# Moving work between VectorE, GpSimd and ScalarE in two mixers of a four-layer network

## The chip, the cores and the metric

The kernel runs on one core of a Trainium2 chip. The metric is the device time of one execution in microseconds, the median of several runs. The engines are TensorE (PE in the profile; PEld is its weight loading), VectorE (DVE), ScalarE (ACT), GpSimd (POOL) and SyncE (SP), which here only issues DMAs. Each runs its own queue of instructions in order and waits on semaphores for the others.

## What is computed

A sequence of 512 tokens of width 1024 passes through four layers in float32. The first two are a block with a gated linear recurrence, then a stick-breaking attention, each followed by a gated feed-forward network; the last two are attention layers with a memory. The change touches the first and the third mixer. Cut to these:

```python
def _rglru_mixer(h, w_in, conv_w, conv_b, w_r, b_r, w_i, b_i, lam, w_out):   # first mixer
    proj = h @ w_in
    gate = gelu(proj[..., :1024], approximate=True)
    xc = causal_depthwise_conv(proj[..., 1024:], conv_w, conv_b)              # four taps
    xg = xc.reshape(bsz, s, 4, 256)
    r = sigmoid(einsum("bsnc,ncd->bsnd", xg, w_r) + b_r)
    i = sigmoid(einsum("bsnc,ncd->bsnd", xg, w_i) + b_i)
    log_a = 8.0 * r * log_sigmoid(lam)
    u = sqrt(maximum(-expm1(2.0 * log_a), 0.0)) * (i * xc)
    hs = linear_scan(exp(log_a), u)
    return (hs * gate) @ w_out

# third mixer: h @ w_in_even gives queries, keys, values of three attentions and a gate
ya = global_gqa(rope(rmsnorm(qa)), rope(rmsnorm(ka)), va)      # 8 heads, 2 key heads
yb = window_gqa(qb, kb, vb, sink_b, rel_bias)                  # 8 heads, 2 key heads
ym = memory_attn(qm, mk, mv)                                   # 4 heads
x = x + (concatenate([ya, yb, ym]) * silu(gate)) @ w_out_even  # each attention: softmax(scores) @ v
```

## The kernel before

Activations lie transposed: a tile is 128 features by 512 tokens. A float32 product is made of three fp32r matmuls: each operand is split into a high part (rounded to fp32r, by ACT) and a low part (operand minus high part), and `mm3` (lines 169 to 171) multiplies high by high, high by low and low by high. A projection of one tile of 128 output features is 24 such matmuls of 512 columns, from two chunks of weights of 128x512.

Weights come through `fetch` (lines 139 to 155): a plan lists all chunks of the whole kernel in the order of their use; the DMA of a chunk goes to one of three buffers `w32`, ACT makes the high part `wh` (line 150), DVE the low part `wl` (line 151), each in one of six buffers. So a chunk can be prepared only up to six chunks ahead of its use, when PE has read the one that had its buffer. The instructions of each engine stand in an order that the framework's scheduler sets from the program; the order within an engine is fixed when the kernel is built.

The first mixer is `rglru`. `RG_STEPS` sets the order of its steps. A step `x` projects two tiles, scales them (DVE, line 423), and convolves each: the first tap by POOL (line 426), three more by DVE (line 429), then a split whose low part POOL makes (line 206). A step `g` multiplies a pair by the two gate matrices (24 matmuls), and then goes between ACT (tanh, exp, square; lines 450 to 463), DVE (lines 462, 464), POOL (maximum with zero, line 465), ACT (square root, with its table load, line 469) and DVE (line 472 and the scan, line 473). A step `y` is a gate tile: a projection, scaled by DVE (479), then the gelu: square on ACT (482), a multiply and add on POOL (483), a product on DVE (484), tanh on ACT (485), and two products on DVE (486, 489), the second with the scan's result; the split's low part is POOL's. The output projection follows with the first seven of the eight tiles, then the eighth.

The third mixer is `even_mixer`. The column tiles of its input weights `we_m` are numbered by `even_col`: 0 is the key of the global attention, 1 to 4 its queries, 5 the key and 6 to 9 the queries of the window attention, 10 to 13 the memory queries, 14 to 17, 18 to 21 and 22 to 25 the gates of the three. A query tile holds two heads. It passes the rope (`rope`; its last addition is POOL's, line 1074), is split (ACT line 204, POOL line 206), and four DMAs stack high and low parts for the score matmuls (lines 551, 552). `gqa_score` computes four blocks of scores per head, their maxima (DVE), the exponentials with their sums (ACT), and `normalise` (lines 961 to 965) multiplies each block by the reciprocal of its sum: four DVE instructions of 128x512 a head. `win_score` does the same with blocks of 256, 384, 384 and 256 columns. PE then transposes the normalised blocks, ACT and DVE split them (lines 620, 621), and PE multiplies them by the values. While a pair of heads is in its softmax, PE projects the next query and a gate tile.

Of the kernel before, what the change touches and what calls it, by code (L numbers as in the profile page):

```python
# [9 lines left out]
F32 = mybir.dt.float32  # L10
F32R = mybir.dt.float32r
BF16 = mybir.dt.bfloat16
AF = mybir.ActivationFunctionType
ALU = mybir.AluOpType
# [51 lines left out]
class Net:  # L66
# [73 lines left out]
    def fetch(self):  # L140
        nc = self.nc
        key, c0, c1 = self.plan[self.fetched]
        self.fetched += 1
        n = c1 - c0
        src = self.a[key[0]][key[1:]][:, c0:c1]
        w = self.w32.get()
        h = self.wh.get()
        l = self.wl.get()
        nc.sync.dma_start(w[:, :n], src)
        nc.scalar.copy(h[:, :n], w[:, :n])  # L150
        nc.vector.tensor_tensor(l[:, :n], w[:, :n], h[:, :n].bitcast(F32), op=ALU.subtract)  # L151
        self.w32.put(w)
        self.wh.put(h)
        self.wl.put(l)
        self.ready.append((key, c0, h, l))

    def weights(self, key, c0=0):

# [212 lines left out]
    def plan_rglru(self):  # L371
# [15 lines left out]
            self.chunks(("w_rgo", k), kd)  # L387

    RG_STEPS = [
        ("x", 0), ("x", 1), ("g", 0), ("x", 2), ("g", 1), ("x", 3), ("g", 2), ("y", 0), ("y", 1),  # L390
        ("g", 3), ("y", 2), ("y", 3), ("y", 4), ("y", 5), ("y", 6), ("y", 7),
    ]

    def first_pair(self, st):
# [15 lines left out]
    def rglru(self, st, gain_next):  # L410
        nc = self.nc
        v, act, pool = nc.vector, nc.scalar, nc.gpsimd
        c = self.scr
        first = deque(self.first_pair(st))
        YH, YL, conv, hs = [], [], {}, {}
        for kind, n in self.RG_STEPS:
            if kind == "x":
                xcs, ch, cl = [], [], []
                for mt in range(2):
                    m = 2 * n + mt  # L420
                    ps = first.popleft() if first else self.proj(("w_rg", 8 + m), st["XH"], st["XL"])
                    xbt, xb = self.f()
                    v.tensor_tensor(xb, ps, self.row(st), op=ALU.mult)
                    self.P.put(ps)
                    xct, xc = self.f()
                    pool.tensor_scalar(xc, xb, self.p("conv_w", 24 + m), self.p("conv_b", m), op0=ALU.mult, op1=ALU.add)
                    for j in (2, 1, 0):
                        d = 3 - j
                        v.scalar_tensor_tensor(xc[:, d:], xb[:, : 512 - d], self.p("conv_w", 8 * j + m), xc[:, d:], op0=ALU.mult, op1=ALU.add)
                    self.F.put(xbt)  # L430
                    xcs.append((xct, xc))
                    h, l = self.split(xc, "p")
                    ch.append(h)
                    cl.append(l)
                conv[n] = xcs, ch, cl
                if n == 0:
                    self.lam_consts()
            elif kind == "g":
                xcs, ch, cl = conv.pop(n)
                tr = []  # L440
                for g in range(2):
                    wh, wl = self.weights(("w_gate4", n), 512 * g)
                    for mt in range(2):
                        m = 2 * n + mt
                        ps = self.P.get()
                        for kt in range(2):
                            s = slice((mt * 2 + kt) * 128, (mt * 2 + kt + 1) * 128)
                            self.mm3(ps, wh[:, s], wl[:, s], ch[kt], cl[kt], kt == 0, kt == 1)
                        tt, t = self.f()
                        act.activation(t, ps, AF.Tanh, scale=0.5, bias=c[:, 16 + 8 * g + m : 17 + 8 * g + m])  # L450
                        self.P.put(ps)
                        tr.append((tt, t))
                self.R.put(*ch, *cl)
                keep = []
                for mt in range(2):
                    m = 2 * n + mt
                    (rt, r), (it, i) = tr[mt], tr[2 + mt]
                    xct, xc = xcs[mt]
                    at, aa = self.f()
                    act.activation(aa, r, AF.Exp, scale=c[:, m : m + 1], bias=c[:, m : m + 1])  # L460
                    act.activation(r, r, AF.Tanh, scale=c[:, 8 + m : 9 + m], bias=c[:, 8 + m : 9 + m])
                    v.scalar_tensor_tensor(i, i, 1.0, xc, op0=ALU.add, op1=ALU.mult)
                    act.square(xc, aa)
                    v.scalar_tensor_tensor(r, xc, 1.0, r, op0=ALU.add, op1=ALU.mult)
                    pool.tensor_scalar(r, r, 0.0, None, op0=ALU.max)
                    self.F.put(xct)
                    keep.append((m, at, rt, it))
                for m, at, rt, it in keep:
                    act.sqrt(rt[:, 0:512], rt[:, 0:512])
                for m, at, rt, it in keep:  # L470
                    r, i = rt[:, 0:512], it[:, 0:512]
                    v.scalar_tensor_tensor(i, i, 0.5, r, op0=ALU.mult, op1=ALU.mult)
                    v.tensor_tensor_scan(r, at[:, 0:512], i, 0.0, op0=ALU.mult, op1=ALU.add)
                    self.F.put(at, it)
                    hs[m] = rt
            else:
                ps = self.proj(("w_rg", n), st["XH"], st["XL"])
                gt, g = self.f()
                v.tensor_tensor(g, ps, self.row(st), op=ALU.mult)
                self.P.put(ps)  # L480
                qt, q = self.f()
                act.square(q, g)
                pool.tensor_scalar(q, q, 0.044715, 1.0, op0=ALU.mult, op1=ALU.add)
                v.tensor_tensor(q, q, g, op=ALU.mult)
                act.activation(q, q, AF.Tanh, scale=0.7978845608028654)
                v.scalar_tensor_tensor(g, q, 1.0, g, op0=ALU.add, op1=ALU.mult)
                self.F.put(qt)
                ht = hs.pop(n)
                v.scalar_tensor_tensor(g, g, 0.5, ht[:, 0:512], op0=ALU.mult, op1=ALU.mult)
                self.F.put(ht)  # L490
                yh, yl = self.split(g, "p")
                self.F.put(gt)
                YH.append(yh)
                YL.append(yl)
# [463 lines left out]
        self.F.put(qt)  # L958
        return hl

    def normalise(self, pieces, sums):
        nc = self.nc
        nc.vector.reciprocal(sums, sums)  # L963
        for c, x in pieces:
            nc.vector.tensor_scalar(x, x, sums[:, c : c + 1], None, op0=ALU.mult)  # L965

    def mem_score(self, q, K):
        nc = self.nc
# [153 lines left out]
    def gqa_score(self, Q, K, r8, hd):  # L1122
        nc = self.nc
        sums = self.small(4)
        tiles, pieces = [], []
        for b in range(4):
# [10 lines left out]
            self.P.put(ps)  # L1137
            tiles.append(t)
            pieces.append((b, p))
        self.normalise(pieces, sums)  # L1140
        return tiles, [x for _, x in pieces]

    def gqa_value(self, W, V):
# [41 lines left out]
    def win_score(self, Q, K, hd):  # L1185

        nc = self.nc
# [26 lines left out]
        es = self.small(4)  # L1214
        nc.scalar.activation(es, neg, AF.Exp, bias=sink)
        nc.vector.tensor_tensor(sums, sums, es, op=ALU.add)
        self.normalise(list(enumerate(xs)), sums)
        return tiles, xs

    def win_value(self, W, V):  # L1220
# [636 lines left out]
```

## Time and profile before

| | before |
|---|---|
| median of 3 runs | 1899.28 us (1898.69 to 1900.81) |
| profiled execution | 1898.13 us, of which the span of the instructions is 1896.1 us |
| PE busy | 1855.3 us, 98% of the span |
| DVE busy | 1204.7 us, 64% |
| ACT busy | 882.5 us, 47% |
| POOL busy | 318.5 us, 17% |

The first mixer lasts until about 153 us after the span's start, the third from about 1200 to 1455 us. PE is busy nearly always, so a change is worth what it does to the short times in which PE isn't, or in which it runs slower. The shares are averages over the whole kernel: in the two mixers DVE is far fuller than 64%.

### The profile page before, as it was taken

How to read it: one execution, taken by the hardware profiler on the slowest of the kernel's cores; microseconds unless marked ns; L12 is line 12 of the kernel's file. 1: busy time of each engine (PE TensorE's matmuls, PEld its weight loads, DVE VectorE, ACT ScalarE, POOL GpSimd, SP SyncE). 2: the span in 40 equal slices, each digit the busy share in tenths (PEclk: the TensorE clock that was granted, in tenths of full speed). 3: DMA queues.
4: the chain of work that ended last, by engine and by line, in shares of the span. 5: the costliest groups of instructions: out<-in, count | busy, mean ns of one | idle time of the engine just before them, and what ended most of it. 6: DMA issues, size and time to landing. Idle time of an engine off the chain costs nothing. (4 is left out here: it accounts for less than half of the span.)

```text
span 1896.1 us, 25818 instructions
## 1 busy us (share of the span) xinstructions
PE 1855.3 (98%) x9003; PEld 1545.3 (81%) x9003; DVE 1204.7 (64%) x2181; ACT 882.5 (47%) x1709; POOL 318.5 (17%) x370
## 2 busy tenths in 40 slices
PE   9899999999999999999999999999999999999998
PEld 6777888888888888788888888788888888888877
DVE  8886555553335998655554335779897665776753
ACT  5764333333334665533333344456665444545542
POOL 3342000000001221200000131222212411322310
PEclk9999999999999999999999999999999999999999
DMA  5333333333335442333333334322443433545532
GB/s 157 101 106 106 95 99 96 97 97 97 94 95 161 135 139 78 94 96 98 97 97 103 104 114 145 89 73 62 112 113 95 129 96 98 145 138 144 142 95 73
DMA packets 124802, 204.04 MB, mean 108 GB/s; under 512 B 21208, under 2 KB 31192, under 8 KB 124672
## 3 DMA queue, kind: packets, MB, share of 16 engines
q1 hardware_dynamic: 124672, 202.39, 37.0%
q8 instruction: 71, 1.16, 0.3%
q14 instruction: 59, 0.48, 0.1%
HBM read 168.76 MB, written 4.40 MB: 91 GB/s over the span
## 5 line engine op out<-in xcount | busy, mean ns | idle before, releaser
L171 PE MATMUL p<-r,wl 128*128 128x512 f32 (+1 forms) x2216 | 853.7, 385 | 10.3 <-DVE wl L151 10.3
L169 PE MATMUL p<-r,wh 128*128 128x512 f32 (+1 forms) x2216 | 856.9, 387 | 2.0 <-ACT wh L150 1.4
L170 PE MATMUL p<-r,wh 128*128 128x512 f32 (+1 forms) x2216 | 852.7, 385 | 3.0 <-POOL r L206 2.2
L150 ACT CAST wh<-w 128x512 fp32r<-128x512 f32 x608 | 371.4, 616 | 643.3 <-PE p L170 480.3
L151 DVE TENSOR_TENSOR wl<-w,wh 128x512 fp32r<-128x512 f32 x608 | 439.9, 727 | 339.4 <-ACT wh L150 337.0
L171 PEld LDWEIGHTS p<-r,wl 128*128 128x128 f32 x2216 | 417.2, 188 | 96.3 <-DVE wl L151 13.9
L169 PEld LDWEIGHTS p<-r,wh 128*128 128x128 f32 x2216 | 417.0, 188 | 86.0 <-ACT wh L150 4.0
L170 PEld LDWEIGHTS p<-r,wh 128*128 128x128 f32 x2216 | 417.3, 188 | 85.6 <-POOL r L206 4.3
L206 POOL TENSOR_TENSOR r<-f,r 128x512 fp32r<-128x512 f32 x102 | 139.5, 1369 | 455.5 <-ACT r L204 454.7
L204 ACT CAST r<-f 128x512 fp32r<-128x512 f32 x146 | 90.7, 621 | 186.2 <-DVE f L532 65.3
L220 POOL TENSOR_TENSOR f<-f,f 128x512 f32<-128x512 f32 x40 | 56.2, 1412 | 478.2 <-ACT f L214 478.0
L506 DVE TENSOR_TENSOR f<-p,f 128x512 f32<-128x512 f32 x68 | 46.9, 690 | 83.5 <-PE p L171 82.8
L621 DVE TENSOR_TENSOR r<-p,r 128x512 fp32r<-128x512 f32 (+2 forms) x152 | 90.4, 638 | 3.7 <-ACT r L620 3.4
L620 ACT CAST r<-p 128x512 fp32r<-128x512 f32 (+2 forms) x152 | 77.2, 558 | 10.5 <-PE p L1152 5.4
L597 PE MATMUL p<-wh,r 128*128 128x512 f32 (+1 forms) x192 | 71.7, 374 | 0.6 <-DVE f L610 0.6
L599 PE MATMUL p<-wh,r 128*128 128x512 f32 (+1 forms) x192 | 71.4, 372 | 0.0
L598 PE MATMUL p<-wl,r 128*128 128x512 f32 (+1 forms) x192 | 71.3, 372 | 0.0
L530 DVE TENSOR_TENSOR f<-p,f 128x512 f32<-128x512 f32 x44 | 30.4, 691 | 63.6 <-PE p L171 63.6
L509 ACT ACTIVATE f<-f 128x512 f32<-128x512 f32 x68 | 43.0, 633 | 38.6 <-DVE f L506 38.5
L682 POOL MEMSET f<- 128x1 f32 x64 | 5.2, 99 | 313.9 <-DVE f L510 208.3
L965 DVE TENSOR_SCALAR f<-f,s 128x256 f32<-128x256 f32 (+3 forms) x160 | 56.5, 416 | 1.1
L683 DVE TENSOR_TENSOR_SCAN f<-f,f 128x127 f32<-128x127 f32 (+3 forms) x64 | 53.1, 870 | 6.3 <-ACT f L676 6.3
(214 smaller groups left out, 1852.9 us busy)
## 6 DMA issues: line engine op xcount, KB each, us to landing
w<-w_gu SPq DMA_DIRECT2D x176, 256.0 KB, 2.9
r<-r SPq DMA_DIRECT2D x240, 128.0 KB, 2.5
w<-w_d SPq DMA_DIRECT2D x80, 256.0 KB, 2.7
w<-wo_m SPq DMA_DIRECT2D x64, 256.0 KB, 2.9
w<-we_m SPq DMA_DIRECT2D x52, 256.0 KB, 2.9
w<-w_rg SPq DMA_DIRECT2D x32, 256.0 KB, 3.0
w<-w_sqk SPq DMA_DIRECT2D x32, 256.0 KB, 2.9
w<-we_o SPq DMA_DIRECT2D x24, 256.0 KB, 2.6
```

Source lines behind the costliest of these rows:

```text
L150: nc.scalar.copy(h[:, :n], w[:, :n])
L151: nc.vector.tensor_tensor(l[:, :n], w[:, :n], h[:, :n].bitcast(F32), op=ALU.subtract)
L169: mm(out, wh, xh, start=start, stop=False)
L170: mm(out, wh, xl, start=False, stop=False)
L171: mm(out, wl, xh, start=False, stop=stop)
L204: nc.scalar.copy(h, src)
L206: e.tensor_tensor(l, src, h.bitcast(F32), op=ALU.subtract)
L597: mm(o, xh, h[:, s], start=st, stop=False)
L598: mm(o, xh, l[:, s], start=False, stop=False)
L599: mm(o, xl, h[:, s], start=False, stop=sp)
L620: nc.scalar.copy(h[:, :n], ps[:, :n])
L621: nc.vector.tensor_tensor(l[:, :n], ps[:, :n], h[:, :n].bitcast(F32), op=ALU.subtract)
```

## The change

Four things. In the first mixer the first tap of the convolution is made by ACT (`Identity` with a scale and a bias for each partition) instead of POOL. The gelu's multiply and add leave POOL: the factor 0.044715 goes into the scale of ACT's square, and the addition of one into DVE's product, which becomes a scalar_tensor_tensor. `RG_STEPS` puts gate tiles between the other steps. In the third mixer the low parts of the weights of column tiles 1 to 9 and 18 to 25 are made by POOL instead of DVE, and one of four blocks of each head is normalised by ACT.

```diff
@@ fetch
-        nc.vector.tensor_tensor(l[:, :n], w[:, :n], h[:, :n].bitcast(F32), op=ALU.subtract)
+        e = nc.gpsimd if self.low_on_pool(key) else nc.vector
+        e.tensor_tensor(l[:, :n], w[:, :n], h[:, :n].bitcast(F32), op=ALU.subtract)
...
+    @staticmethod
+    def low_on_pool(key):
+
+        return key[0] == "we_m" and (1 <= key[1] <= 9 or key[1] >= 18)
@@ RG_STEPS
-        ("x", 0), ("x", 1), ("g", 0), ("x", 2), ("g", 1), ("x", 3), ("g", 2), ("y", 0), ("y", 1),
-        ("g", 3), ("y", 2), ("y", 3), ("y", 4), ("y", 5), ("y", 6), ("y", 7),
+        ("x", 0), ("x", 1), ("g", 0), ("y", 0), ("x", 2), ("g", 1), ("y", 1), ("y", 2), ("x", 3),
+        ("g", 2), ("y", 3), ("y", 4), ("g", 3), ("y", 5), ("y", 6), ("y", 7),
@@ rglru, step x
-                    pool.tensor_scalar(xc, xb, self.p("conv_w", 24 + m), self.p("conv_b", m), op0=ALU.mult, op1=ALU.add)
+                    act.activation(xc, xb, AF.Identity, scale=self.p("conv_w", 24 + m), bias=self.p("conv_b", m))
@@ rglru, step y
-                act.square(q, g)
-                pool.tensor_scalar(q, q, 0.044715, 1.0, op0=ALU.mult, op1=ALU.add)
-                v.tensor_tensor(q, q, g, op=ALU.mult)
+                act.activation(q, g, AF.Square, scale=0.044715**0.5)
+                v.scalar_tensor_tensor(q, q, 1.0, g, op0=ALU.add, op1=ALU.mult)
@@ normalise
-    def normalise(self, pieces, sums):
+    def normalise(self, pieces, sums, act=None):
...
-            nc.vector.tensor_scalar(x, x, sums[:, c : c + 1], None, op0=ALU.mult)
+            if c == act:
+                nc.scalar.activation(x, x, AF.Copy, scale=sums[:, c : c + 1])
+            else:
+                nc.vector.tensor_scalar(x, x, sums[:, c : c + 1], None, op0=ALU.mult)
@@ gqa_score
-        self.normalise(pieces, sums)
+        self.normalise(pieces, sums, 3)
@@ win_score
-        self.normalise(list(enumerate(xs)), sums)
+        self.normalise(list(enumerate(xs)), sums, 2)
```

Lines stand further down in the changed kernel: one or two in `fetch`, five or six in `rglru`, eight in the rope.

The order of the queues moves with it. First DVE in the first mixer, where the first step `g` ends. Before, with the taps of `x` 2 among it (line 423 the evacuation, 429 the taps, 464, 472 and 473 the gate instructions and scans, `wl` the weights' low parts):

```order
L423 TENSOR_TENSOR f_210<-p_116,f_212 128x512
L429 SCALAR_TENSOR_TENSOR f_211<-f_210,par,f_211 128x511
L464 SCALAR_TENSOR_TENSOR f_202<-f_213,f_202 128x512
L429 SCALAR_TENSOR_TENSOR f_211<-f_210,par,f_211 128x510
L464 SCALAR_TENSOR_TENSOR f_205<-f_215,f_205 128x512
L429 SCALAR_TENSOR_TENSOR f_211<-f_210,par,f_211 128x509
L151 TENSOR_TENSOR wl_234<-w_2_222,wh_228 128x512
L151 TENSOR_TENSOR wl_229<-w_0_220,wh_223 128x512
L472 SCALAR_TENSOR_TENSOR f_206<-f_206,f_202 128x512
L472 SCALAR_TENSOR_TENSOR f_207<-f_207,f_205 128x512
L473 SCALAR_TENSOR_TENSOR f_202<-f_208,f_206 128x512
L473 SCALAR_TENSOR_TENSOR f_205<-f_209,f_207 128x512
```

In the changed kernel (470, 478, 479 are the gate instructions and scans, 429 the evacuation of `x`, 435 its taps, 485, 489, 491 and 494 a gate tile):

```order
L485 TENSOR_TENSOR f_210<-p_116,f_212 128x512
L470 SCALAR_TENSOR_TENSOR f_202<-f_213,f_202 128x512
L470 SCALAR_TENSOR_TENSOR f_205<-f_215,f_205 128x512
L489 SCALAR_TENSOR_TENSOR f_211<-f_211,f_210 128x512
L478 SCALAR_TENSOR_TENSOR f_206<-f_206,f_202 128x512
L478 SCALAR_TENSOR_TENSOR f_207<-f_207,f_205 128x512
L479 SCALAR_TENSOR_TENSOR f_202<-f_208,f_206 128x512
L479 SCALAR_TENSOR_TENSOR f_205<-f_209,f_207 128x512
L429 TENSOR_TENSOR f_204<-p_117,f_212 128x512
L491 SCALAR_TENSOR_TENSOR f_210<-f_211,f_210 128x512
L152 TENSOR_TENSOR wl_234<-w_2_222,wh_228 128x512
L494 SCALAR_TENSOR_TENSOR f_210<-f_210,f_202 128x512
```

The first gate tile's instructions stand where taps of `x` 2 stood, the evacuation of `x` 2 follows the scans, and its taps come further down, with `wl` between them.

Then POOL in the third mixer, at the second and third query tiles of the global attention. Before (1074 the rope's addition, 206 the low parts of a query and of an output, 239 a power for the norm):

```order
L1074 TENSOR_TENSOR f_218<-f_218,f_209 128x512
L206 TENSOR_TENSOR r_166<-f_218,r_177 128x512
L239 TENSOR_TENSOR s_106<-s_105,mhalf 128x8
L206 TENSOR_TENSOR r_154<-f_209,r_155 128x512
L1074 TENSOR_TENSOR f_207<-f_207,f_203 128x512
```

In the changed kernel (1082, 212 and 245 are the same three, 152 the weights' low parts):

```order
L1082 TENSOR_TENSOR f_217<-f_217,f_203 128x512
L152 TENSOR_TENSOR wl_230<-w_1_221,wh_224 128x512
L152 TENSOR_TENSOR wl_231<-w_2_222,wh_225 128x512
L212 TENSOR_TENSOR r_158<-f_217,r_177 128x512
L152 TENSOR_TENSOR wl_232<-w_0_220,wh_226 128x512
L245 TENSOR_TENSOR s_106<-s_105,mhalf 128x8
L212 TENSOR_TENSOR r_154<-f_203,r_155 128x512
L152 TENSOR_TENSOR wl_233<-w_1_221,wh_227 128x512
L1082 TENSOR_TENSOR f_216<-f_216,f_204 128x512
```

Four low parts of weights a query stand on POOL, two of them here between the rope's addition and the query's low part.

## Rows read from the trace of the kernel before

**Rows 1.** Windows: stretch, length, busy us (instructions) of PE, PEld, DVE, ACT, POOL; PEclk

```profile
25.00:150.00 125.00, 115.38 (x489) 91.95 (x488) 106.73 (x155) 80.25 (x128) 52.73 (x40) 0.99 0.33 99
79.00:82.50 3.50, 3.50 (x10) 2.70 (x9) 2.59 (x5) 2.13 (x4) 1.27 (x2) 0.51 0.72 195
1258.00:1432.00 174.00, 168.46 (x881) 140.41 (x879) 162.44 (x383) 111.47 (x266) 35.74 (x25) 1.00 0.33 91
```

**Rows 2.** Waits of PE, 25 to 153 us: us in total, times, longest

```profile
PE p L171 <- DVE wl L151: 6.9, 4, 3.7
PE p L170 <- POOL r L206: 1.9, 2, 1.0
```

**Rows 3.** Timeline of PE: start, us, what, [idle before <- who ended it]

```profile
78.05 0.50 PE L171 MATMUL p<-r,wl 128*128 128x512 f32 x1 [3.69 <-DVE wl L151]
...
79.55 0.63 PE L170 MATMUL p<-r,wh 128*128 128x512 f32 x1
79.98 0.63 PE L171 MATMUL p<-r,wl 128*128 128x512 f32 x1
```

**Rows 4.** Waits of DVE, 25 to 150 us

```profile
DVE f L429 <- POOL f L426: 6.6, 8, 2.0
DVE f L484 <- POOL f L483: 3.4, 4, 1.9
DVE f L464 <- ACT f L463: 2.4, 4, 0.8
DVE f L472 <- ACT f L469: 2.1, 3, 1.0
```

**Rows 5.** Timeline of DVE in the first mixer

```profile
73.21 0.75 DVE L429 SCALAR_TENSOR_TENSOR f<-f,par,f 128x511 f32<-128x511 f32 x1 [2.00 <-POOL f L426]
...
75.08 2.33 DVE L473 TENSOR_TENSOR_SCAN f<-f,f 128x512 f32<-128x512 f32 x2
77.33 0.67 DVE L151 TENSOR_TENSOR wl<-w,wh 128x512 fp32r<-128x512 f32 x1
...
82.03 1.76 DVE L429 SCALAR_TENSOR_TENSOR f<-f,par,f 128x511 f32<-128x511 f32 x1 [0.91 <-POOL f L426]
...
98.44 1.28 DVE L151 TENSOR_TENSOR wl<-w,wh 128x512 fp32r<-128x512 f32 x2
...
124.73 1.10 DVE L489 SCALAR_TENSOR_TENSOR f<-f,f 128x512 f32<-128x512 f32 x1
```

**Rows 6.** Timeline of POOL in the first mixer

```profile
81.96 1.29 POOL L206 TENSOR_TENSOR r<-f,r 128x512 fp32r<-128x512 f32 x1
```

**Rows 7.** Groups of ACT, 25 to 150 us: count, busy us, mean ns

```profile
L482 ACT ACTIVATE f<-f 128x512 f32<-128x512 f32 x8 | 5.0, 630 | 3.3 <-DVE f L479 3.3
```

**Rows 8.** Waits of PE, 1240 to 1456 us

```profile
PE p L1129 <- DMA r<-r: 2.3, 2, 1.2
PE p L1163 <- DVE r L621: 1.1, 2, 0.7
PE p L1230 <- DVE f L965: 1.1, 2, 0.8
PE p L1241 <- DVE r L621: 0.9, 3, 0.4
```

**Rows 9.** Timeline of DVE in the third mixer

```profile
1259.10 1.41 DVE L151 TENSOR_TENSOR wl<-w,wh 128x512 fp32r<-128x512 f32 x1
...
1270.43 1.68 DVE L965 TENSOR_SCALAR f<-f,s 128x512 f32<-128x512 f32 x4
...
1425.47 1.27 DVE L1192 TENSOR_TENSOR f<-f,f 128x384 f32<-128x384 f32 x1
```

**Rows 10.** Waits of DVE, 1240 to 1455 us

```profile
DVE wl L151 <- ACT wh L150: 5.7, 4, 3.9
```

**Rows 11.** Timeline of POOL in the third mixer

```profile
1280.90 1.28 POOL L206 TENSOR_TENSOR r<-f,r 128x512 fp32r<-128x512 f32 x1 [0.73 <-ACT r L204]
```

## The prediction, made before the changed kernel ran

> **What bounds the kernel now.** I read the windows first. TensorE (PE) is the long pole, yet in two stretches it loses time: in the first mixer, from 25 to 150 us, it is busy 115.38 of 125 us, and in the third mixer, from 1258 to 1432 us, 168.46 of 174 [rows 1]. Both are the stretches in which VectorE (DVE) is fullest: 106.73 of 125 and 162.44 of 174 [rows 1]. So the second view is who made PE wait there.
>
> In the first mixer it is nearly all one thing: the low part `wl` of a weight chunk, written by DVE, 6.9 us in four waits, and 1.9 us for a low part made by GpSimd (POOL) [rows 2]. The largest wait, 3.69 us, ends at 78.05 [rows 3]. The DVE timeline tells why that `wl` is late [rows 5]: it runs at 77.33, and ahead of it in DVE's queue stand a convolution step that sat 2.00 us for POOL's first tap (73.21) and two scans (75.08, 2.33 us). The weights themselves are there. PE waits because DVE, an in-order queue, waits for POOL. In all DVE waits 6.6 us for POOL's convolution tap (L426), 3.4 us for POOL's gelu step (L483), and 4.5 us for ScalarE (ACT) results in the gate steps [rows 4]. Busy 106.7 and waits 14.5 make 121 of 125 us: DVE is the bound of this stretch, and PE follows it.
>
> There is a second cost. From 79.0 to 82.5 us, right after the 3.69 us in which PE did nothing, the granted clock is 0.51, the lower of its two levels (1.2 GHz), and from one matmul to the next it is 0.43 us (79.55 to 79.98 [rows 3]), where the stretch has 115.38 / 489 = 0.24 on the mean [rows 1]. Eight matmuls by 0.20 us are 1.6 us. PE's loss in the stretch is so 9.6 + 1.6 = 11.2 us, and that is the most that anything done for DVE can give back here (a few tenths of restart after each wait aside).
>
> In the third mixer the waits are small and of several kinds: 2.3 us for the DMA that stacks a query tile, 1.1 and 0.9 us for DVE's transposed low parts (L621), 1.1 us for DVE's normalised scores (L965) [rows 8].
>
> **The change, part by part: first mixer.** POOL loses 16 instructions, the eight first taps and the eight gelu steps. The taps go to ACT as eight activations; the nearest row is a 128x512 activation from SBUF, 0.630 us [rows 7], so ACT gets 5.0 us more on 80.25 of 125 [rows 1]. The gelu step is folded into the square's scale and DVE's next instruction, which becomes a scalar_tensor_tensor of the same shape and number: nothing.
>
> On DVE's chain: the waits for L426 and L483 go, 6.6 + 3.4 = 10.0 us [rows 4]. POOL's gelu step also held DVE up while it ran: the instruction at 124.73 takes 1.10 us instead of some 0.7 [rows 5]; there are four such, together 1.5 us. Against that, the tap on ACT can make DVE wait too: between nothing and eight times 0.63 = 5.0 us. I take 1.0, near the lower end, because in the new order there stand one to three other DVE instructions between the evacuation and the first step that reads the tap (0.6 us or more; two `wl` in a row take 1.28 us, so 0.60 each [rows 5]). DVE's chain: -10.0 - 1.5 + 1.0 = -10.5 us.
>
> The gate tiles spread: PE is asked for the same matmuls in another order. A gate tile asks PE for 24 matmuls, 5.5 us at 0.23, and DVE for four instructions and two `wl`, some 4 us; `x` and `g` of one block ask PE for 72, 16.5 us, and DVE for six `wl`, two evacuations, six taps, six gate instructions and two scans, some 16 us by the durations of [rows 5]. Before, the latter came nearly in one piece, and six gate tiles behind the last `g` or just ahead of it; now a gate tile or two stand after each `g`. This removes no DVE work; it keeps PE fed while DVE does the scans. I cost it at nothing by itself. Its risk is at the end, where only three gate tiles instead of six lie behind the last `g` for DVE to catch up in. That cover is worth 1.5 us a tile (5.5 less 4); if it is missing, the last gate tile's low part would be late at the output projection, and the saving be less by what DVE is behind.
>
> So the stretch ends 10.5 us earlier by DVE and at most 11.2 by PE. The two are then about equally late and jostle each other, so I take -10.0. Ends: -2.0 (the first rival) and -13 (with the restarts).
>
> **Third mixer.** 34 low parts (17 column tiles of `we_m` by two chunks) go from DVE to POOL: DVE loses 34 x 0.60 = 20.4 us. Sixteen normalisings go to ACT: eight of 128x512 at 0.40 (four in a row take 1.68 us [rows 9]), 3.2 us, and eight of 128x384 at some 0.30, 2.4 us. Together 26.0 us off DVE. ACT gets 16 x 0.6 = 10 us on 111.47 of 174 [rows 1] and has room.
>
> But POOL's work isn't free for DVE. At 82.03 a convolution step takes 1.76 us instead of 0.75, because POOL's two-input subtraction started at 81.96 and runs 1.29 us [rows 5, 6]. In 1258 to 1432 fifteen DVE instructions are held like that, the first at 1259.10 (1.41 us, where a `wl` takes 0.67 at 77.33 [rows 5]), the last at 1425.47 (1.27) [rows 9]; together 11.4 us, beside 21 two-input POOL instructions: 0.54 us each. None of the fifteen reads PSUM. By that average the 34 new ones give back 34 x 0.54 = 18.4 us, so DVE is relieved by 26.0 - 18.4 = 7.6 us only, to about 155 of 174. The Trainium skill, page "SBUF — State Buffer", section "Who interferes with whom", states that a DVE instruction with two SBUF inputs and a GpSimd one that reads SBUF exclude each other for a whole instruction. The rows of 82.03 agree; taken for each of the 34 it would cost far more than my average, and it is a rival below.
>
> What of it reaches PE: the waits for DVE, 1.1 + 1.1 + 0.9 = 3.1 us [rows 8], go at best. Against that stands POOL's queue. In the new order one or two `wl` stand between the rope addition and the subtraction that makes a query's low part. Before, the subtraction at 1280.90 starts 0.73 us after that addition [rows 11], and the stacking DMA waits for it; one `wl` between costs 1.29 - 0.73 = 0.6 us, two 1.9 us. Two of nine stacks already made PE wait (2.3 us [rows 8]); I add four times 0.4 = 1.6 us. Third mixer: -3.1 + 1.6 = -1.5. Ends: -5.4 (all four waits gone) and +12 (the third rival).
>
> **Sum.** The profiled execution took 1898.13 us: 1898.1 - 10.0 - 1.5 = 1886.6. It lies 1.15 us under the median of the runs, 1899.28, against which the change is timed: 1888.
>
> **The rivals.**
> 1. The waits move instead of going. The gate steps still wait for POOL's maximum, a table load and the square root; those 4.5 us [rows 4] double, since the convolution steps that stood between them now stand elsewhere, and the tap on ACT is exposed in full (+4.0 on my 1.0). First mixer -2.0, total 1896. For it: the two gate instructions and the scaled sum stand closer together in the new order. Against: other DVE work was waiting anyway and now fills these waits.
> 2. Everything goes: the first mixer at its ceiling with the restarts, -13, and all 5.4 us of the third: 1881. For it speaks that PE's waits in the third mixer are short; against it that POOL's queue gets longer there.
> 3. Each new POOL instruction holds DVE for its whole length: 34 x 1.29 = 43.9, less 26.0, is +17.9 us on DVE, 180 us of work for a stretch of 174. The stretch grows by 6 (DVE without any idle time) to 18 us, say 12: 1901, no change. For it: the longest holds are 1.0 to 1.1 us. Against: DVE's evacuations, row maxima and score sums there read PSUM, and none of them is among the fifteen. The rule of the Trainium skill, page "SBUF — State Buffer", section "Who interferes with whom", would have it so wherever DVE has two operands in SBUF.
> 4. Slower: POOL's queue. A `wl` is issued behind its high part on ACT, which waits for a free buffer; DVE's longest such wait was 3.9 us [rows 10]. On POOL the same wait stands in front of a query's or key's low part, whose DMA and score matmuls follow. Nine stacks, each 3.9 late with some 1.5 us of slack, are 9 x 2.4 = 21.6 us: 1898.1 - 10 - 3.1 + 21.6 + 1.15 = 1908. It ends slower than before once a stack is on average over 3.2 us late. Against: the waited-for high parts stand ahead of the split on ACT in only part of the steps.
>
> **How the numbers follow.** Forecast 0.64 (its own range 1883 to 1893), rival 1 0.12, rival 2 0.08, rival 3 0.09, rival 4 0.07. A measurement of this kernel tells 0.2%, 3.8 us, from no change, so under 1895.5 counts as faster: 0.64 + 0.08 + half of rival 1 = 0.78. Within 0.2%: the other half of rival 1 and most of rival 3, 0.13. Slower: 0.09. The range takes in rivals 1 and 2 and leaves out 3, 4 and the tail of 1: 1880 to 1897.
>
> **What would show it.** Right: between 25 and 150 us PE's waits for `wl` fall from 6.9 to under 2, no stretch of half clock near 80 us, DVE's waits for L426 and L483 absent and not replaced by over 2 us for the tap on ACT. In the third mixer POOL busy by some 44 us more, DVE's held instructions up from fifteen to about 40, PE's waits for the transposed low parts and the normalised scores down, those for the stacking DMA up a little. Wrong: a new wait of PE at the end of the first mixer for the last gate tile, or score matmuls that wait over 3 us for their DMA.

## The result, and the profile after

The changed kernel takes 1913.74 us in the median (1908.75 to 1914.52), the kernel before 1899.00 in the same series: a ratio of 1.0072, interval 1.006 to 1.0085. It is 0.7% slower, where 1888 was forecast. Its profiled execution took 1914.39 us.

| | before | after |
|---|---|---|
| span of the profiled execution | 1896.1 us | 1912.6 us |
| PE busy | 1855.3 us, 98% | 1866.9 us, 98% |
| DVE busy | 1204.7 us, 64% | 1186.7 us, 62% |
| ACT busy | 882.5 us, 47% | 897.1 us, 47% |
| POOL busy | 318.5 us, 17% | 345.1 us, 18% |

DVE is relieved by 18.0 us and the kernel is 16.5 us longer in the trace. Where it was lost is told by the start of the same matmul in both traces (each has 9003, and from the 601st on, behind the first mixer's projections, they stand in the same order but for a few dozen in the third mixer). The difference is worked out from the two starts:

```
start, us        before    after   after - before
601st matmul      156.0    154.0    -2.0   (first mixer)
5501st           1204.0   1203.5    -0.5   (up to the third mixer)
6201st           1346.8   1357.8   +11.0   (global attention's steps)
7001st           1506.2   1520.8   +14.6   (window attention's steps)
last             1888.9   1905.4   +16.5
```

So the first mixer gains 2.0 us of the forecast 10, and the third loses 15.1 where it was to gain 1.5. The rest, some 3 us behind the first mixer's end and behind the third's, is for the most part two stretches at the lower clock that the trace of before doesn't have, at 1201 and 1829 us, some 1.5 us each (between 1190 and 1258 us the mean granted clock is 0.97, before 1.00).

The windows that answer to [rows 1] (start:end, length, busy time of PE, PE's weight loading, DVE, ACT and POOL with counts, granted clock, DMA share, GB/s), of the changed kernel:

```profile
25.00:150.00 125.00, 117.89 (x500) 95.92 (x499) 106.90 (x159) 88.64 (x139) 36.43 (x24) 0.96 0.33 101
1258.00:1450.00 192.00, 178.64 (x896) 146.37 (x896) 150.15 (x348) 122.89 (x289) 71.96 (x53) 0.97 0.30 84
```

In the third mixer DVE is no longer full: 150 of 192 us, before 162 of 174. Yet PE lost more, so DVE's work wasn't what it lost it to. PE's waits there, which answer to [rows 8] (L1171 and L1137 are the L1163 and L1129 of before):

```profile
PE p L1171 <- DVE r L626: 8.3, 7, 2.2
...
PE p L1137 <- DMA r<-r: 1.0, 1, 1.0
```

The first was 1.1 us, the second 2.3. PE multiplies transposed scores by values there and waits for their low parts, which DVE makes. DVE's own waits between 1258 and 1450 us, of the kernel before and of the changed one, tell why those are late (waiting line, releaser: us in total, times, longest):

```profile
DVE s L1095 <- POOL s L239: 3.4, 4, 1.2
```

```profile
DVE s L1103 <- POOL s L245: 17.5, 4, 4.9
DVE s L1224 <- ACT s L1223: 7.1, 8, 1.5
```

One small instruction, 128x8: DVE multiplies the power that POOL made for a query's norm (`rstd`, L245) by 0.125 (L1103 in `gqa_q`). Once in each of four steps DVE stands still for it. The DVE timeline of one step of the changed kernel (start, duration, instruction, count, idle time before it and what ended that):

```profile
1309.14 0.68 DVE L511 TENSOR_TENSOR f<-p,f 128x512 f32<-128x512 f32 x1
1309.74 0.15 DVE L243 TENSOR_SCALAR s<-p 128x8 f32<-128x8 f32 x1
1314.80 0.17 DVE L1103 TENSOR_SCALAR s<-s 128x8 f32<-128x8 f32 x1 [4.92 <-POOL s L245]
1314.88 0.68 DVE L626 TENSOR_TENSOR r<-p,r 128x512 fp32r<-128x512 f32 x1
```

And POOL's timeline in the same step:

```profile
1306.90 1.30 POOL L1082 TENSOR_TENSOR f<-f,f 128x512 f32<-128x512 f32 x1 [1.81 <-DVE f L1080]
1308.15 1.29 POOL L152 TENSOR_TENSOR wl<-w,wh 128x512 fp32r<-128x512 f32 x1
1309.40 1.29 POOL L212 TENSOR_TENSOR r<-f,r 128x512 fp32r<-128x512 f32 x1
1310.65 2.51 POOL L152 TENSOR_TENSOR wl<-w,wh 128x512 fp32r<-128x512 f32 x2
1313.12 1.65 POOL L245 TENSOR_TENSOR s<-s,mhalf 128x8 f32<-128x8 f32 x1
```

DVE's input for the power is there at 1309.89. Three new low parts and the split's subtraction stand ahead of the power in POOL's queue, which starts it at 1313.12. Behind the multiplication, in DVE's queue, stand the low parts of the transposed scores. PE stops for them, and when it goes on it is slow; its timeline, cut:

```profile
1315.62 0.50 PE L1171 MATMUL p<-r,r 128*128 128x512 f32 x1 [2.10 <-DVE r L626]
...
1316.82 0.50 PE L1171 MATMUL p<-r,r 128*128 128x512 f32 x1 [0.47 <-DVE r L626]
...
1318.44 0.63 PE L1171 MATMUL p<-r,r 128*128 128x512 f32 x1
1318.87 0.63 PE L1137 MATMUL p<-r,r 128*128 128x512 f32 x1
```

From 1318.02 to 1320.6 matmuls start 0.43 us apart instead of 0.23: the granted clock is 0.50 there, the lower of the two levels, seven matmuls by 0.2, 1.4 us. With the 2.57 us of waiting that is 4.0 us, and such steps follow each other at 27.4 us (1288.15, 1315.62, 1343.03) where they followed at 23.3 before. Three such steps make about the 11 us.

In the first mixer, PE's waits between 25 and 153 us, which answer to [rows 2]:

```profile
PE p L177 <- DVE wl L152: 6.0, 3, 2.3
PE p L175 <- ACT wh L150: 1.1, 1, 1.1
```

Three waits instead of four, and the last, 2.3 us at 130.58, is followed by 13 matmuls at the lower clock (131 to 137 us: granted 0.56). DVE's waits there answer to [rows 4]:

```profile
DVE f L478 <- ACT f L475: 5.5, 8, 1.2
DVE f L470 <- ACT f L469: 3.4, 4, 1.6
DVE wl L152 <- ACT wh L150: 3.1, 5, 1.2
...
DVE f L435 <- ACT f L432: 1.4, 3, 0.9
```

The waits for POOL are gone; those for ACT's square roots and squares (L475, L469), 4.5 us before, are 8.9. The 2.0 us are of this one trace: in three others with the same first mixer (e1_first, e6_unqueued and e7_r8pool, below) the 601st matmul starts 3.5 to 4.0 us earlier than before.

### The profile page after: what moved, and what is told of

The parts are those of the page before. It is cut to its first block, busy times and chain, and to the rows that moved or that the text cites. A ratio compares the mean times of both kernels' runs of the same rounds, so it can differ in the third digit from the quotient of the medians.

```text
span 1912.6 us, 25803 instructions
## 1 busy us (share of the span) xinstructions
PE 1866.9 (98%) x9003; PEld 1554.3 (81%) x9003; DVE 1186.7 (62%) x2131; ACT 897.1 (47%) x1733; POOL 345.1 (18%) x388
## 5 line engine op out<-in xcount | busy, mean ns | idle before, releaser
L152 DVE TENSOR_TENSOR wl<-w,wh 128x512 fp32r<-128x512 f32 x574 | 414.4, 725 | 339.8 <-ACT wh L150 338.8
L177 PEld LDWEIGHTS p<-r,wl 128*128 128x128 f32 x2216 | 418.4, 189 | 95.1 <-DVE wl L152 12.1
L973 DVE TENSOR_SCALAR f<-f,s 128x256 f32<-128x256 f32 (+2 forms) x144 | 57.0, 456 | 1.2
```

The costliest lines, as they stand in the source:

```text
L152: e.tensor_tensor(l[:, :n], w[:, :n], h[:, :n].bitcast(F32), op=ALU.subtract)
L177: mm(out, wl, xh, start=False, stop=stop)
```

## Experiments: the third mixer

Three theories of the third mixer's loss stood at first. Q: the low parts delay the power in POOL's queue. H: DVE is held while POOL subtracts. A: the normalisings delay ACT's queue.

**The two parts of the change, each alone.** e1_first has of the change's diff the lines of `rglru` and `RG_STEPS`, e2_third those of `fetch`, `low_on_pool` and `normalise`; one line of each is shown:

```diff
 e1_first
+                    act.activation(xc, xb, AF.Identity, scale=self.p("conv_w", 24 + m), bias=self.p("conv_b", m))
 e2_third
+        e = nc.gpsimd if self.low_on_pool(key) else nc.vector
```

> The kernel before with the first mixer's part of the change alone (order of the gate tiles, first tap on ScalarE, gelu step folded). Theory S (the gain was smaller than forecast by itself: in the changed kernel the first mixer was 2.0 us shorter): about 1897, 1895 to 1899. Rival M (the first mixer's part is worth its forecast 10 us, and what the changed kernel shows there is disturbed by the other part): 1889. PE's waits for low parts between 25 and 153 us: S about 6.0 us as in the changed kernel, M under 2.

> The kernel before with the third mixer's part alone (34 low parts on GpSimd, sixteen normalisings on ScalarE). The changed kernel's trace puts the loss there: 11.9 us in the stage of the first four query tiles, 2.7 in the next four. If that is all this part's doing: 1899 + 14.6 = 1913 to 1915. If half of it comes from the position of the half-clock stretches, which the first part shifts: about 1906.

Measured: the first part 1898.65 us, ratio 0.9993 (0.9983 to 1.0003): nothing, or up to 3 us gained; PE still waits 6.5 us for low parts. The third part 1911.75, 1.0064 (1.0049 to 1.0079), +12.1 us. The third part makes the loss, and the first has no gain to set against it. The two differences add up to +11.1, the changed kernel measured +14.7; the intervals (some 2 us on the first part, 3 on the third, 2 on the changed kernel) about cover the 3.6 us that are missing.

**The queue of the power.** First, 11 low parts back on DVE (e6_unqueued):

```diff
-        e = nc.gpsimd if self.low_on_pool(key) else nc.vector
+        e = nc.gpsimd if self.low_on_pool(key) and (key[1], c0) not in self.NOT_POOL else nc.vector
...
+    NOT_POOL = {(3, 0), (3, 512), (4, 0), (4, 512), (5, 0), (5, 512), (6, 512),
+                (19, 512), (20, 512), (21, 0), (21, 512)}
```

> The changed kernel with 11 of its 34 low parts back on VectorE: those that stand in GpSimd's queue between a query's rope addition and the power for that query's norm. Theory Q (those low parts delay the power; VectorE, in order, waits 17.5 us in 4 for it instead of 3.4, and TensorE waits 8.3 us behind and then runs at half clock): VectorE's wait for the power back under 5 us, TensorE's wait for the transposed low parts under 2.5 us, 1901 to 1903. Theory H (VectorE held while GpSimd's subtractions run): a third of the holds goes, 1911 to 1913. Theory A (the normalisings on ScalarE delay the high parts and the transposed tiles): no change, 1913 to 1914.

Then all low parts left on POOL, and the waiting instruction taken out of DVE's queue (e7_r8pool):

```diff
-            self.nc.vector.tensor_scalar(r8, factors(), 0.125, None, op0=ALU.mult)
+            self.nc.gpsimd.tensor_scalar(r8, factors(), 0.125, None, op0=ALU.mult)
```

> The changed kernel with one small instruction moved: the 0.125 on the query's norm factors (128x8) goes from VectorE to GpSimd, right behind the power it reads, so that VectorE's queue no longer stands still for the power; all 34 low parts stay on GpSimd. Theory Q: VectorE's 17.5 us wait goes, a later one for the factors themselves of at most 1 us a step in its place, 1900 to 1903. Theories H and A: 1912 to 1914.

Measured: 1903.28 (1.0016, interval 1.0006 to 1.0025) and 1897.82 (0.9991, 0.9981 to 1.0000), 10 and 16 us less than the changed kernel; Q had asked for 1900 to 1903 in the second. One instruction of 128x8 on another engine gives back as much as the third mixer had lost. By the starts of the matmuls it does so in the global attention alone: its steps (5501st to 6201st) take 139.1 us, in the changed kernel 154.3, before 142.7, and both H and A are out as the main cause there. The window attention's (to the 7001st) still take 163.3 us, in the changed kernel 163.0, before 159.5: that loss has another cause, and the two cancel. The waits of DVE for the power and of PE for the low parts in the first of the two runs, and of PE in the second, where DVE has no wait for the power:

```profile
DVE s L1106 <- POOL s L248: 2.3, 4, 0.9
```

```profile
PE p L1174 <- DVE r L629: 4.0, 7, 1.0
```

```profile
PE p L1171 <- DVE r L626: 1.1, 1, 1.1
```

In the first, PE's wait did not fall under the 2.5 us that Q asked for. POOL's timeline in the second shows that nothing else was moved: the low parts are ahead of the power as before, it is as late, and now only POOL waits for it.

```profile
1302.79 3.01 POOL L152 TENSOR_TENSOR wl<-w,wh 128x512 fp32r<-128x512 f32 x2
1305.76 1.66 POOL L245 TENSOR_TENSOR s<-s,mhalf 128x8 f32<-128x8 f32 x1
1307.51 0.24 POOL L1103 TENSOR_SCALAR s<-s 128x8 f32<-128x8 f32 x1
```

**The third part's two halves.** The normalisings alone (e3_norm: block 3 of each head in the global, block 2 in the window attention) and the low parts alone (e5_low, with `low_on_pool` as in the change).

```diff
 e3_norm
+            if c == act:
+                nc.scalar.activation(x, x, AF.Copy, scale=sums[:, c : c + 1])
 e5_low
+        e = nc.gpsimd if self.low_on_pool(key) else nc.vector
```

> The kernel before with the sixteen normalisings on ScalarE alone; all low parts stay on VectorE. Theory Q (the third mixer's loss is the low parts in front of the power in GpSimd's queue and nothing else): no loss here, 1897 to 1900, VectorE's wait for the power at about 3.4 us as before. Theory A (the normalisings delay ScalarE's queue): over 1903.

> The kernel before with the 34 low parts on GpSimd alone. The whole third part cost 12.1 us, the normalisings alone 2.9. If the two add up: 1908 to 1909. If the normalisings on ScalarE in part offset the harm (VectorE's own normalisings are what GpSimd's subtractions hold): 1911 to 1914.

Measured: 1902.55 (1.0021, 1.0011 to 1.0030) and 1914.34 (1.0077, 1.0062 to 1.0092). Neither Q nor A had the first right: the normalisings do cost some 3 us by the medians and 4 by the ratio, less than A asked for. PE waits for ACT's exponentials, which it doesn't in the kernel before. The ACT timeline of e3_norm at one of the three places, and PE's row there:

```profile
1291.62 0.62 ACT L204 CAST r<-f 128x512 fp32r<-128x512 f32 x1 [2.23 <-DVE f L1031]
1292.14 0.77 ACT L1139 ACTIVATE f<-p,s,s 128x512 f32<-128x512 f32 x1
```

```profile
1293.06 0.50 PE L169 MATMUL p<-r,wh 128*128 128x512 f32 x1 [0.60 <-ACT f L1139]
```

In the kernel before the first exponential runs ahead of that cast, which waits for a gate product (L1028, the L1031 of e3_norm):

```profile
1290.52 0.78 ACT L1136 ACTIVATE f<-p,s,s 128x512 f32<-128x512 f32 x1 [1.64 <-DVE s L1134]
...
1291.78 0.62 ACT L204 CAST r<-f 128x512 fp32r<-128x512 f32 x1 [0.39 <-DVE f L1028]
```

With the normalisings on ACT the cast stands first in its queue. The three waits are 1.8 us of the loss; the rest of it is spread and left open. The low parts alone cost 15.5 us, 3 more than with the normalisings on ACT, which the two intervals hardly tell from nothing. It would fit if beside POOL's subtractions it is DVE's normalisings that are held, and the rows show that they are. The DVE and POOL timelines of e5_low in a step of the window attention:

```profile
1404.89 0.68 DVE L971 TENSOR_SCALAR f<-f,s 128x384 f32<-128x384 f32 x2
...
1406.66 4.40 DVE L971 TENSOR_SCALAR f<-f,s 128x256 f32<-128x256 f32 x4
```

```profile
1406.80 1.36 POOL L152 TENSOR_TENSOR wl<-w,wh 128x512 fp32r<-128x512 f32 x1 [4.32 <-ACT wh L150]
1408.13 1.41 POOL L212 TENSOR_TENSOR r<-f,r 128x512 fp32r<-128x512 f32 x1
1409.51 1.40 POOL L152 TENSOR_TENSOR wl<-w,wh 128x512 fp32r<-128x512 f32 x1
```

Two of them free take 0.68 us, four (of 256 and 384 columns) beside three subtractions 4.40 instead of some 1.4: each subtraction held one back by about 1.0 us. These instructions have a single tensor in SBUF as input. The Trainium skill, page "SBUF — State Buffer", section "Who interferes with whom", has such `tensor_scalar` instructions among those that can use the port pair shared with GpSimd, which one of the two then holds for a whole instruction; the row agrees.

**Low parts without the queue.** On a better base (tap and gelu step moved, old order of the gate tiles, 0.125 on POOL: b1_r8), all 34 low parts (b2_low) and only those that are loaded during the global attention (b3_gqa); no normalisings on ACT.

```diff
 b3_gqa against b2_low
-        return key[0] == "we_m" and (1 <= key[1] <= 9 or key[1] >= 18)
+        return key[0] == "we_m" and (1 <= key[1] <= 5 or 18 <= key[1] <= 21)
```

> The kernel before with the first tap on ScalarE, the gelu step folded, the old order of the gate tiles, and the 0.125 on the query's norm factors on GpSimd; nothing else of the third mixer's part. The first two alone gave 1892.4; VectorE's four waits for the power, 3.4 us, go with the third, and of TensorE's waits for the transposed low parts 1.1 us at most: 1890 to 1892.

> The previous kernel plus the 34 low parts on GpSimd, without the normalisings on ScalarE. Theory Q alone (the low parts harmed only through the power's queue): 1887 to 1890, since VectorE is relieved and no longer waits for GpSimd. Theory QH (they also hold VectorE's normalisings of the windowed scores, where in the changed kernel three of them took 3.03 us): about 3.5 us gained in the stage of the first four query tiles and 2 to 4 lost in the next, 1890 to 1893.

> As the previous one, but with low parts on GpSimd only for the tiles that are loaded in the stage of the first four query tiles (columns 1 to 5 and 18 to 21, 18 low parts of 34). Theory QH: the gain of the first stage stays, the loss of the next goes, 1887 to 1889. Theory Q alone: half of the gain goes, 1889 to 1891.

Measured: 1892.56 (0.9957, 0.9940 to 0.9973), 1899.47 (0.9996, 0.9985 to 1.0008), 1891.70 (0.9958, 0.9945 to 0.9970). Moving the 0.125 is worth nothing by itself (1892.41 without it, below): DVE's 3.4 us for the power weren't on PE's path. The 34 low parts cost 7 us more even with the power's queue out of the way, where at most a small gain was expected; the 18 of them that are loaded in the global attention cost nothing and gain nothing. So the other sixteen cost some 8 us, and they stand where the rows above show the holds: there theory H has its place. In the traces 4.8 us of it lie between the 6201st and the 7001st matmul (165.2 us in b2_low, 160.4 in b3_gqa), and PE's waits there are 5.9 us against 2.5; the largest two of b2_low are for transposed tiles:

```profile
PE p L1246 <- DVE r L626: 2.1, 5, 0.7
PE p L1167 <- ACT r L625: 1.3, 1, 1.3
```

That the holds are all of the 8 us is not shown.

## Experiments: the first mixer

**Tap and gelu step alone, order alone.** e4_tap_gelu has the change's tap and gelu lines and the old `RG_STEPS`; e8_steps has the new `RG_STEPS` only.

```diff
 e4_tap_gelu
+                    act.activation(xc, xb, AF.Identity, scale=self.p("conv_w", 24 + m), bias=self.p("conv_b", m))
+                act.activation(q, g, AF.Square, scale=0.044715**0.5)
 e8_steps: before, after
-   x0 x1 g0 x2 g1 x3 g2 y0 y1 g3 y2 y3 y4 y5 y6 y7
+   x0 x1 g0 y0 x2 g1 y1 y2 x3 g2 y3 y4 g3 y5 y6 y7
```

> The kernel before with the first tap on ScalarE and the gelu step folded, the old order of the gate tiles. VectorE's waits for GpSimd's tap and gelu step, 10.0 us, go. Theory O (the new order of the gate tiles eats the gain): 1890 to 1893. Theory B (the gain is small in itself, since TensorE waits for low parts that stand behind two scans, and those wait for ScalarE's square roots, whatever else is removed): 1895 to 1898, and TensorE's waits for low parts between 25 and 153 us still over 4 us.

> The kernel before with the new order of the gate tiles alone. Theory O: slower than before by 5 us or more, 1904. Theory B: 1897 to 1901.

Measured: 1892.41 (0.9961, 0.9946 to 0.9976), a gain of 7.2 us, and 1903.36 (1.0019, 1.0010 to 1.0029), a loss of 3.7. With both it was 1898.65: on top of the other edits the new order takes 6 us back. That is theory O, though alone the order costs less than the 5 us that O asked for. The 601st matmul starts at 148.2 us in the first, 159.7 in the second and 152.0 with both. PE's waits between 25 and 153 us, with the old order and with the new one:

```profile
PE p L171 <- DVE wl L151: 3.9, 3, 2.1
```

```profile
PE p L171 <- DVE wl L151: 6.5, 3, 2.3
```

What a wait looks like with the new order, DVE's timeline of e1_first and PE's row (L472 is the product with the square root, L473 the scans):

```profile
76.19 0.69 DVE L472 SCALAR_TENSOR_TENSOR f<-f,f 128x512 f32<-128x512 f32 x1 [0.56 <-ACT f L469]
76.80 2.33 DVE L473 TENSOR_TENSOR_SCAN f<-f,f 128x512 f32<-128x512 f32 x2
79.05 0.67 DVE L151 TENSOR_TENSOR wl<-w,wh 128x512 fp32r<-128x512 f32 x1
```

```profile
79.77 0.50 PE L171 MATMUL p<-r,wl 128*128 128x512 f32 x1 [2.32 <-DVE wl L151]
```

The low part that PE waits for stands behind the scans, and those behind two square roots that ACT makes after a table load. That pattern is in the old order too, where PE waits 1.4 us at the first such place instead of 2.3.

**Which part of the order.** Three orders on the base b1_r8: the late last gate alone (f1_late_gate), the early gate tiles with the last two gates in a row (f2_early_tiles), the early gate tiles without that (f3_early_tiles2).

```diff
 f1   x0 x1 g0 x2 g1 x3 g2 y0 y1 y2 y3 y4 g3 y5 y6 y7
 f2   x0 x1 g0 y0 x2 g1 y1 y2 x3 g2 g3 y3 y4 y5 y6 y7
 f3   x0 x1 g0 y0 x2 g1 y1 x3 g2 y2 y3 g3 y4 y5 y6 y7
```

> Tap on ScalarE, gelu step folded, 0.125 on GpSimd (1892.6 with the old order of the gate tiles), and of the new order only its end: five gate tiles between the third gate and the last, three behind it. Theory E (the late last gate costs the 6 us): 1897 to 1899. Theory P (the gate tiles right behind the early gates cost them): 1891 to 1893.

> The same base, and of the new order only its beginning: one gate tile right behind the first gate and two behind the second, the last gate right behind the third, five tiles behind it. Theory P: 1896 to 1899. Theory E: 1890 to 1893.

> Tap on ScalarE, gelu step folded, 0.125 on GpSimd, and one gate tile right behind the first gate, one behind the second, two behind the third, four behind the last. Theory P (a gate tile right behind a gate costs, since its low parts and its own steps stand behind two scans that wait for the square roots): 1896 to 1898, TensorE's waits for low parts between 25 and 153 us above 5 us. If the cost came only from the two gates in a row: 1891 to 1893.

Measured: 1893.56 (0.9969, 0.9958 to 0.9981), 1896.81 (0.9988, 0.9979 to 0.9997), 1893.88 (0.9970, 0.9957 to 0.9983), against 1892.56 of the base. The second has a fault of its own, a wait for the inputs of the last gate:

```profile
PE p L169 <- ACT r L204: 3.3, 2, 2.0
```

The first and the third cost some 2 us each by the ratio, which their intervals hardly tell from nothing. So no single place of the order was found that costs the 6 us; that both ends share in it is likely and not shown. Theory P, that early gate tiles cost it by themselves, is out by the third run, though the first two had about fitted it.

**Scans behind the next projection.** Each gate's square roots and scans are issued behind the next projection's matmuls, on the changed kernel with the 0.125 on POOL (e9_defer) and on b1_r8 (b4_defer):

```diff
-                for m, at, rt, it in keep:
-                    act.sqrt(rt[:, 0:512], rt[:, 0:512])
...
+                late.append(keep)
...
                 ps = self.proj(("w_rg", n), st["XH"], st["XL"])
+                scans()
```

> The changed kernel with the 0.125 on GpSimd (1898 by itself) and, in the first mixer, each gate's two square roots and two scans issued behind the matmuls of the next projection instead of in front of them, so that the low parts of that projection stand ahead of the scans in VectorE's queue. Theory B: TensorE's three waits of about 2 us behind the scans go, and with them the half-clock stretches there, together 9 us: 1889 to 1891. Rival: the scans are then late for the gate tiles that read them and the waits only move: 1896 to 1900.

> The first kernel of this group plus the square roots and scans of each gate issued behind the matmuls of the next projection, with the old order of the gate tiles. If TensorE's remaining waits behind the scans (3.9 us in 3 in the first mixer) go and no new ones come: 1886 to 1888. If what keeps TensorE waiting there is VectorE's whole work and not its order: 1890 to 1893.

Measured: 1893.88 (0.9964, 0.9953 to 0.9976) and 1889.69 (0.9949, 0.9931 to 0.9968). Against the same kernels without it (1897.82 and 1892.56) that is 3.9 and 2.9 us, about half of the hope; the second lies within the intervals. The waits behind the scans get shorter, but PE still waits for low parts, 3.5 us in three in e9_defer. So the order of DVE's queue is part of the cause. That its amount of work is the rest fits, and is not shown.

**The best of it.** b4_defer with, in the global attention only, the low parts on POOL (`low_on_pool` as in b3_gqa) and the fourth block normalised by ACT.

```diff
 b5_gqa_all against b4_defer
+        return key[0] == "we_m" and (1 <= key[1] <= 5 or 18 <= key[1] <= 21)
-        self.normalise(pieces, sums)
+        self.normalise(pieces, sums, 3)
```

> The best so far (tap, gelu step, 0.125 on GpSimd, square roots and scans behind the next projection: 1889.7) plus, in the stage of the first four query tiles only, the low parts on GpSimd and one normalising in four on ScalarE. In the changed kernel with the 0.125 moved, that stage was 1.9 us shorter than without both: 1887 to 1889. If the low parts' holds cost as much as VectorE is relieved: 1889 to 1891.

Measured: 1887.72 (0.9939, 0.9927 to 0.9951), the fastest, 0.6% faster than before and 1.3% than the change as it was made. Its lead of 2 us on b4_defer is within the intervals. PE's waits between 25 and 153 us in it, together 4.0 us, in the kernel before 9.5 and a stretch of lower clock:

```profile
PE p L177 <- DVE wl L152: 2.5, 2, 1.8
PE p L175 <- ACT wh L150: 1.0, 1, 1.0
PE p L176 <- POOL r L212: 0.5, 2, 0.3
```

## Why the prediction was wrong

**What bounds the kernel: right.** Low parts behind waiting DVE instructions in the first mixer; small waits of many kinds in the third.

**Tap and gelu step, -10 on the chain: right in kind, and too large.** The 10.0 us of waits for POOL went, and alone these edits gained 7.2 us (7.8 in the trace). The tap on ACT made DVE wait 1.4 us, where 1.0 was taken; it has a scale and a bias for each partition and lasts 0.82 us, not 0.63:

```profile
L432 ACT ACTIVATE f<-f,par x8: 802/817/818, 26.2 to 94.2; 128x512 f32<-128x512 f32 x8
```

(Nanoseconds of the changed kernel's taps: shortest, median, longest.)

**Gate tiles spread, "I cost it at nothing by itself": the first failed term.** It costs 6 us beside the other edits and 3.7 alone. The count of work by step was no help, since it took DVE as busy all the time; the first rival had seen that the waits for ACT would double, and they did (4.5 to 8.9 us). It gave the first mixer -2.0, which is what the changed trace shows, but in part by luck: its tap exposed in full did not come (1.4 us of 5.0), and other traces of the same first mixer show -3.5 to -4.0. Nor is that doubling the cause by itself: with the old order and the other edits the same waits are 7.6 us, and the gain stays. The half clock that was to go at 80 us went in the changed kernel's trace, and another stretch came at 131; in that of e7_r8pool, with the same first mixer, it is there (79 to 83 us: granted 0.59).

**Third mixer, "what of it reaches PE": the second failed term, and the larger.** -1.5 forecast, +12.1 measured. The working looked for what stands behind the low parts in POOL's queue, and found the query's split and its DMA: those were no later (PE's wait for that DMA fell from 2.3 to 1.0 us). It didn't list the other POOL instruction of each step, the 128x8 power of the norm, for which the kernel before already made DVE wait 3.4 us, nor what is queued on DVE behind that wait. The runs put 16 us on it: with the one DVE instruction that waits for the power moved to POOL, that much is gone (e7_r8pool). So the fourth rival had the right queue, POOL's, and the wrong rest: it had low parts that wait there for ACT's high parts, in front of the split, where in the row above POOL runs without a pause and the subtractions' own time delays the power. That its 1908 comes near is luck. Its bound doesn't come out of its own sum either: nine stacks cancel the 13.1 us of gain when they are on average 3.0 us late, not 3.2.

**The holds, 0.54 us an operation: too simple.** With the normalisings on ACT the new operations held DVE less than forecast: over 1258 to 1450 us the DVE instructions that ran beside a POOL one were longer than usual by 17.5 us in some 20 cases, before 11.4 in fifteen; about 40 cases were forecast. The average hid two cases: beside a normalising a POOL subtraction costs 1.0 us, elsewhere often nothing, and none of the instructions that were held reads PSUM. Where the subtractions meet the normalisings, in the window attention, the sixteen low parts cost more than they relieved, which b2_low against b3_gqa shows and the third rival foresaw in kind.

**"ACT has room": the third failed term, 3 to 4 us.** By busy time it has (122.89 of 192). But ACT's queue changes its order, and the exponentials that free PSUM come later (e3_norm). The rows show 1.8 us of that, and only with the low parts left on DVE.

**What would show it.** PE's waits for `wl` fell to 6.0, not under 2; a stretch of half clock remained; DVE's tap wait was below 2 us as asked. In the third mixer POOL got its work, outside the first mixer 43 us more, but PE's wait for low parts rose instead of falling. The signs named for "wrong", a late last gate tile and late score matmuls, did not appear: the harm came through an instruction that the prediction doesn't name.

## What to carry to other kernels

Before work is put on an engine that looks idle, list every instruction that already stands in its queue in that stage, the smallest too, and for each who waits for it and what is queued behind that waiter: a 128x8 instruction between two in-order queues cost 16 us here, and the 34 large ones that were moved gained nothing even without that cost. Where such a short result crosses engines and goes on, let the engine that makes it also make its next step, so that no full queue stands still for it; while POOL's queue was short, that was worth nothing (b1_r8). And time the parts of a change one by one: here a gain of 7 us was hidden behind a reordering that cost 6 and a move that cost 12 to 15.

## What the runs showed of the hardware

A wait of PE can cost more than itself: the three waits of 2.1 to 2.2 us at 1288, 1315 and 1343 us, each with another of 0.5 behind it, were followed by some 1.4 us lost to matmuls 0.43 us apart, the lower clock. But not always: the wait of 1.99 us at 110.26 in the changed kernel and that of 2.32 at 79.77 in e1_first were followed by matmuls at the usual 0.23, while those of 2.04 at 109.31 and 2.11 at 129.63 in e1_first were followed by slow ones. Executions of one kernel differ by several us (1908.75 to 1914.52 for the changed kernel), which such stretches would explain in part, though no run here shows it; the trace of e1_first is of an execution 3.4 us under its median.
